# Encoder block on one core: the last round of the second MLP product by plain block products, and first operands loaded in order of use

## The chip, the cores and the metric

The kernel runs on one core of a Trainium2 chip, in one launch. The metric is the device time in microseconds, the median of several executions. Engines: TensorE (PE, with PEld for its weight loads), VectorE (DVE), ScalarE (ACT), GpSimd (POOL) and SyncE (SP), which issues most of the transfers.

## What is computed

The reference is one layer of a hybrid encoder block for 1024 rows of 1024 features in f32: a grouped-query attention branch and a state-space branch, merged and added to x, and then an MLP. Only the end of the MLP is changed here:

```python
h2 = rms_norm(x, norm2_w[l]) * (1.0 + scale2) + shift2
ff = jnp.square(jax.nn.relu(h2 @ w_mlp1[l])) @ w_mlp2[l]
x = x + gate2 * ff
```

`w_mlp1` is 1024 x 4096 and `w_mlp2` 4096 x 1024. The second product thus has 1024 rows, an inner length of 4096 and 1024 columns; each of its rows is gated by column and added to the residual x.

## The kernel before, in words

**Exact products.** An f32 operand is split in two: `hi`, cast by ACT (L169), and `lo`, source less `hi`, by DVE (`tt` in `split`, printed as L155, the line of the helper that records every such operation). A product is then three matmuls: hi by hi, hi by lo, lo by hi (L1672 to L1674 in the second MLP product).

**First MLP product.** The 4096 inner features are 16 pairs `p` of 2 x 128. For each pair the result, 256 features by 1024 rows, is seen as 2 x 2 blocks of 128 x 512 and computed by seven products (`product`, L1331 to L1333) in the manner of Strassen and Winograd, put together by DVE. `keep` applies the squared relu and stores the blocks in DRAM, as `r_d[p][b]`: A11, A12 and A22; POOL forms four sums of blocks, S1 to S4 (`a_sum`), which are stored too.

**Second MLP product.** NR = 4 rounds of KR = 4 pairs. In each round the same seven-product scheme is used, in the order 1, 5, 6, 7, 2, 3, 4: product p takes a block or sum of A (`A_OF`, read back from `r_d`) and a block or sum of the weights, where B11, B12, B21, B22 are read from `w2` and the sums are formed by POOL in place (`SY` is the slot of the sums). A product is 4 steps k (one for each pair of the round) of 4 row blocks t of 3 matmuls, into four PSUM banks, and two sets of four banks take turns. So a round has 7 x 4 x 4 x 3 = 336 matmuls, the whole 1344. In round 0 ACT copies the banks to accumulators `acc[p, t]` (printed as `ac`); in the later rounds DVE adds them. `prepare(n)` makes the two split operands of step n, LA = 2 steps ahead of the matmuls, and sends the next transfers: `a_load` into a ring of 16 tiles `ar`, `load` into the slots `sl`. Split operands (printed as `o`) go round in 12 slots (`op_ring`).

**The end of it.** In the last round `combine` turns the sums of the products into the four output blocks, row half by column half. `gated` multiplies by gate2 and adds the residual tile `xl`, both on POOL for all four blocks (`CE`, "G" each). Where a product is the last of a block, DVE multiplies its bank by the gate into `pg`, adds it, and `finish` sends the tile out.

**The order.** Tiles are allocated from pools with a fixed number of buffers, and a scheduler with a model of the engines fixes the order of the instructions on each engine from the program; a transfer into a reused slot waits for that slot's last reader. The slots `ar` and B12's are those of the first product's operands (pool `act`, 32 of them), so they come free towards its end.

Of the kernel before, what the change touches and what calls it, by code (L numbers as in the profile page):

```python
# [18 lines left out]
P = 128  # L19
# [28 lines left out]
LA = 2  # L48
LA0 = 2
CE = ("GG", "GG", "GG", "GG")  # L50
# [41 lines left out]
def block(ctx: ExitStack, tc: tile.TileContext, ia, out, upto=99, dbg=None):  # L92
# [33 lines left out]
    r_d = [[dram(f"r_{p}_{b}", [P, 512]) for b in range(7)] for p in range(DFF // P // 2)]  # L126
# [1218 lines left out]
    def act_tile(name):  # L1345
        return act.tile([P, 512], F32, name=name, tag="act", bufs=32)

    B11, B21 = act_pairs("b11"), act_pairs("b21")
    with tc.tile_pool(name="p6", bufs=1, reuse_waits="tile") as p6:
# [60 lines left out]
        B22, T1 = act_pairs("b22"), act_pairs("t1")  # L1410
# [19 lines left out]

    with tc.tile_pool(name="p7", bufs=1, reuse_waits="tile") as p7:


        A11, A12, A22, S1, S2, S3, S4 = range(7)
# [19 lines left out]
        def first_two(p, ps1, ps2):  # L1454
            c1 = p7.tile([P, 512], F32, name="c1", tag="c1", bufs=NPRE) if p < NPRE else cu("c1")
# [37 lines left out]
        def load(rd, b, k):  # L1493
            if rd < NR:
                q, h = src[b]
                i = 2 * (rd * KR + k) + q
                dma(blk(b, k), w2[i * P:(i + 1) * P, h * 512:(h + 1) * 512])

        A_OF = {1: A11, 5: S1, 6: S2, 7: S3, 2: A12, 3: S4, 4: A22}
        aloaded = [0]  # L1500
# [9 lines left out]
        ORDER = (1, 5, 6, 7, 2, 3, 4)  # L1510
        steps = [(rd, p, k) for rd in range(NR) for p in ORDER for k in range(KR)]
        ready = {}

        def operand(x, e_lo):
            t = next(op_ring)()
            split(t[:, 0], t[:, 1], x, e_lo=e_lo)
            return t

        def prepare(n):
# [3 lines left out]
            g = lambda b: blk(b, k)  # L1523
            if p == 1:
                b = g(B11_)
            elif p == 5:
                b = g(SY)
                tt(G, b, g(B12_), g(B11_), ALU.subtract)
            elif p == 2:
                b = g(B21_)  # L1530
            elif p == 6:
                b = g(SY)
                tt(G, b, g(B22_), b, ALU.subtract)
            elif p == 7:
                b = g(B12_)
                tt(G, b, g(B22_), b, ALU.subtract)
            elif p == 3:
                b = g(B22_)
            else:
                b = g(B21_)  # L1540
                tt(G, b, g(SY), b, ALU.subtract)
# [20 lines left out]
        raws = {0: load_raw(0)}  # L1562
        for p in range(NP):
# [36 lines left out]
            keep(p, None, b21)  # L1600
# [8 lines left out]
    aring.extend(act_tile("ar") for k in range(4))  # L1609
    for b in (SY, B22_, B21_):  # L1610
        slots[b] = [act_tile("sl") for k in range(KR)]
    for b in (B22_, B21_):
        for k in range(KR):
            load(0, b, k)
    with tc.tile_pool(name="p8", bufs=1, reuse_waits="tile") as p8:
# [7 lines left out]
        def gated(t, h, c, v, e1, e2):  # L1623

            cs = slice(c * 512, (c + 1) * 512)
            xl = p8.tile([P, 512], F32, name="xl", tag="xl", bufs=4)
# [99 lines left out]
```

## Time and profile before

| | us |
|---|---|
| median of 3 runs | 2586.99 (2585.14 to 2591.76) |
| profiled execution | 2585.15 |
| its span | 2583.3 |

The page's mean granted TensorE clock is 0.975. The second MLP product fills the last 355 us of the span, from 2229. A profile is read here by stretches: busy time of an engine in a stretch, then what each of its instructions waited for. A row of the time line gives start, length, engine, line, operation, output and inputs, and in brackets the idle time before it and what ended it. PE's matmuls are pipelined: the distance between two starts is what one costs, not the length printed.

### The profile page before, as it was taken

To read this page: it belongs to the slowest core of one execution; us is meant where nothing else is said; L and a number is where in the kernel's file an instruction comes from. 1 tells how busy PE (TensorE), PEld (TensorE's weight loads), DVE (VectorE), ACT (ScalarE), POOL (GpSimd) and SP (SyncE) were. 2 spreads that over 40 slices of the span, in tenths; PEclk is the share of its full clock that TensorE was granted. 3 is DMA by queue.
4 is the path that set the end of the run, shared out by engine and by line. 5 is a ranking of instruction groups with operands and counts; after the bars stand their busy time and mean duration, and the time that the engine had idled before them with its cause. 6 is when DMAs were issued, how large, how long until landed. Compare 5 with 4: busy or idle time off the path is not lost.

```text
span 2583.3 us, 32423 instructions
## 1 busy us (share of the span) xinstructions
PE 2435.1 (94%) x11355; PEld 1942.7 (75%) x11355; DVE 1835.2 (71%) x2175; ACT 1135.0 (44%) x1968; POOL 1047.2 (41%) x760
## 2 busy tenths in 40 slices
PE   5999999999989999999899999998989999899995
PEld 5898777777767777777577767776867888688884
DVE  5756446888856666666577786557569888768889
ACT  5455423544456666666333444344232222364440
POOL 3210117776611111110356665424028756533356
PEclk9999999999999999999899999999999999899998
DMA  7653751333531212111766665476325443754422
GB/s 262 179 164 123 238 169 59 93 94 91 177 119 58 84 51 95 52 56 37 250 200 193 199 193 172 125 233 208 106 77 178 169 156 139 281 162 152 143 89 98
DMA packets 285619, 369.68 MB, mean 143 GB/s; under 512 B 34057, under 2 KB 166897, under 8 KB 285457
## 3 DMA queue, kind: packets, MB, share of 16 engines
q1 hardware_dynamic: 213873, 292.56, 36.2%
q10 hardware_dynamic: 71584, 75.06, 8.7%
q8 instruction: 90, 1.47, 0.2%
q14 instruction: 72, 0.59, 0.1%
HBM read 251.33 MB, written 116.20 MB: 142 GB/s over the span
## 4 chain that ended last, share of the span: by engine, by line
PE 69%; DVE 11%; DMA 8%; issue 5%; POOL 3%; ACT 3%; SPq 1%; ACTq 0%; DVEq 0%; POOLq 0%
PE pst L905 5%; PE pp L1331 4%; PE pp L1333 4%; PE pp L1332 4%; PE psg L207 4%; PE psg L208 4%; PE psg L209 3%; PE psq L381 3%; PE psq L382 3%; PE psq L380 3%; PE p L1673 3%; PE p L1674 3%; PE p L1672 3%; DVE cacc L714 3%; PE pss L888 2%
## 5 line engine op out<-in xcount | busy, mean ns | idle before, releaser
L892 DVE TENSOR_REDUCE nm<-pss 128x1 f32<-128x1024 f32 x128 | 156.7, 1225 | 134.9 <-PE pss L890 133.4
L381 PE MATMUL psq<-twl,hh 128*128 128x400 f32 (+1 forms) x512 | 193.8, 380 | 5.7 <-DVE twl L155 4.9
L1673 PE MATMUL p<-o,o 128*128 128x512 f32 x448 | 179.6, 401 | 19.2 <-DVE o L155 19.2
L380 PE MATMUL psq<-twh,hh 128*128 128x400 f32 (+1 forms) x512 | 193.4, 383 | 3.3 <-ACT hh L306 1.3
L382 PE MATMUL psq<-twh,hl 128*128 128x400 f32 (+1 forms) x512 | 192.8, 378 | 0.0
L894 ACT ACTIVATE pf<-pss,nm 128x1024 f32<-128x1024 f32 x128 | 142.8, 1116 | 102.0 <-PE pst L905 99.2
L155 DVE TENSOR_TENSOR pl<-pst,ph 128x512 fp32r<-128x512 f32 x256 | 167.9, 683 | 27.7 <-ACT ph L169 27.7
L1672 PE MATMUL p<-o,o 128*128 128x512 f32 x448 | 177.8, 401 | 8.5 <-ACT o L169 8.3
L1674 PE MATMUL p<-o,o 128*128 128x512 f32 x448 | 177.0, 397 | 0.0
L155 POOL TENSOR_TENSOR av<-av,rz 64x512 f32<-64x512 f32 x32 | 41.2, 1288 | 326.7 <-DMA rz<-rz 167.6
L905 PEld LDWEIGHTS pst<-masks,pf 128*128 128x128 f32 x1024 | 118.4, 140 | 69.9 <-issue 29.6
L169 ACT CAST ph<-pst 128x512 fp32r<-128x512 f32 x256 | 146.4, 585 | 54.2 <-PE pst L905 40.9
L905 PE MATMUL pst<-masks,pf 128*128 128x128 f32 x1024 | 157.1, 276 | 11.7 <-DVE pl L155 9.6
L155 POOL TENSOR_TENSOR sl<-sl 128x512 f32<-128x512 f32 x64 | 94.7, 1487 | 176.6 <-DVE o L155 82.2
L714 DVE SCALAR_TENSOR_TENSOR cacc<-pad,cwT,cacc 128x1024 f32<-128x1024 f32 x96 | 162.9, 1727 | 0.4
L169 ACT CAST o<-ar 128x512 fp32r<-128x512 f32 x112 | 69.7, 623 | 175.1 <-PE p L1674 155.8
L155 DVE TENSOR_TENSOR o<-ar,o 128x512 fp32r<-128x512 f32 x112 | 108.1, 965 | 49.3 <-ACT o L169 49.3
L169 ACT CAST wop<-ws 128x512 fp32r<-128x512 f32 x116 | 71.4, 621 | 106.1 <-PE pp L1333 69.2
L1673 PEld LDWEIGHTS p<-o,o 128*128 128x128 f32 x448 | 86.4, 193 | 42.0 <-DVE o L155 24.5
L381 PEld LDWEIGHTS psq<-twl,hh 128*128 128x128 f32 x512 | 99.2, 194 | 17.5 <-DVE twl L155 5.5
L380 PEld LDWEIGHTS psq<-twh,hh 128*128 128x128 f32 x512 | 98.6, 193 | 15.7 <-ACT qkvr L513 1.6
L155 DVE TENSOR_TENSOR o<-sl,o 128x512 fp32r<-128x512 f32 x112 | 108.6, 970 | 0.1
(417 smaller groups left out, 7200.8 us busy)
## 6 DMA issues: line engine op xcount, KB each, us to landing
ar<-r SPq DMA_DIRECT2D x112, 256.0 KB
wada<-in_w_ada_dram SPq DMA_DIRECT2D x48, 512.0 KB
r<-in_w_mlp_dram SPq DMA_DIRECT2D x32, 512.0 KB
r<-as SPq DMA_DIRECT2D x64, 256.0 KB
sl<-in_w_mlp_dram SPq DMA_DIRECT2D x64, 256.0 KB
r<-in_w_in_dram SPq DMA_DIRECT2D x26, 512.0 KB
r<-ro ACTq DMA_DIRECT2D x48, 256.0 KB
xb<-cst ACTq DMA_DIRECT2D x20, 512.0 KB
```

The source lines that it names most:

```text
L155: e.tensor_tensor(out=o, in0=a, in1=b, op=op)
L169: (e_hi or A.copy)(hi, src)
L380: T.matmul(o, hhi[k][half][:, sl], hi[:, k % 2, :n], start=k == 0, stop=False)
L381: T.matmul(o, hhi[k][half][:, sl], lo[:, k % 2, :n], start=False, stop=False)
L382: T.matmul(o, hlo[k][half][:, sl], hi[:, k % 2, :n], start=False, stop=k == KT - 1)
L714: V.scalar_tensor_tensor(out=acc, in0=pad[:, k:k + S], scalar=cwT[:, 24 * k + i:24 * k + i + 1], in1=acc, op0=ALU.mult, op1=ALU.add)
L892: V.tensor_reduce(out=nm, in_=ps, axis=AX.X, op=ALU.max, negate=True)
L894: A.activation(pfs[u], ps, AF.Exp, bias=nm, accum_out=zall[:, u:u + 1])
L905: T.transpose(pt[:, k], pf[:, (hf * 4 + k) * P:(hf * 4 + k + 1) * P], ident)
L1672: T.matmul(pss[t], a[:, 0, sl], b[:, 0], start=k == 0, stop=False)
L1673: T.matmul(pss[t], a[:, 0, sl], b[:, 1], start=False, stop=False)
L1674: T.matmul(pss[t], a[:, 1, sl], b[:, 0], start=False, stop=k == KR - 1)
```

## The change

- The last round uses eight plain block products: for each row half h, inner half q and column half c one, 4 steps of 12 matmuls each, 384 matmuls in place of 336. All eight PSUM banks belong to one row half. The last two of a half's eight steps are done bank by bank, and each bank is finished (gate product, addition, output transfer) as soon as it is full. A fourth block, A21, is kept in `r_d` for the pairs of this round, and their sums S1 to S4 aren't formed.
- `so_far` combines the sums of rounds 0 to 2, applies the gate and adds the residual, on DVE, beside the last round. `gated`, `combine` and `CE` go.
- First operands: four tiles `afirst` in a pool of their own, loaded with B11 during the first product; then B12 and the tiles of the second product in turns, then B22 and those of the third. The sums of weights in round 0 are formed by DVE, in rounds 1 and 2 by POOL. LA is 3. Of the split slots 8 (`HOLD`) are used again for the last round's first weights.

```diff
-LA = 2
+LA = 3
 LA0 = 2
-CE = ("GG", "GG", "GG", "GG")
...
-    r_d = [[dram(f"r_{p}_{b}", [P, 512]) for b in range(7)] for p in range(DFF // P // 2)]
+    r_d = [[dram(f"r_{p}_{b}", [P, 512]) for b in range(8)] for p in range(DFF // P // 2)]
...
-        B22, T1 = act_pairs("b22"), act_pairs("t1")
+        T1, B22 = act_pairs("t1"), act_pairs("b22")
...
+    c1p = ctx.enter_context(tc.tile_pool(name="c1p", bufs=1, reuse_waits="tile"))
...
-        slots, aring = {}, []
+        slots, afirst, aring = {}, [], []
...
+        ORDER = (1, 5, 6, 7, 2, 3, 4)
+        PLAIN = {"00": A11, "01": A12, "10": A21, "11": A22}
+        A_OF = {1: A11, 5: S1, 6: S2, 7: S3, 2: A12, 3: S4, 4: A22, **PLAIN}
+        steps = [(rd, p, k) for rd in range(NR) for p in (ORDER if rd < NR - 1 else PLAIN) for k in range(KR)]
+        aloaded, ready, plain_a, plain_b = [0], {}, {}, {}
+
+        def a_tile(n):
+            return afirst[n] if n < KR else aring[(n - KR) % RING]
 
         def a_load(upto):
 
-            while aloaded[0] < min(upto, len(steps) if len(aring) == RING else len(aring)):
+            while aloaded[0] < min(upto, len(steps) - len(PLAIN) * KR):
                 n = aloaded[0]
                 rd, p, k = steps[n]
-                dma(aring[n % RING], r_d[rd * KR + k][A_OF[p]])
+                dma(a_tile(n), r_d[rd * KR + k][A_OF[p]])
...
+        def plain_load(*names):
+
+            for nm in names:
+                for k in range(KR):
+                    if nm in PLAIN:
+                        plain_a[nm, k] = act_tile("ar")
+                        dma(plain_a[nm, k], r_d[(NR - 1) * KR + k][PLAIN[nm]])
+                    else:
+                        slots[nm][k] = act_tile("sl")
+                        load(NR - 1, nm, k)
...
+            e = V if rd == 0 else G
+            if p in PLAIN:
+                ready[n] = operand(plain_a[p, k], more_slot)
+                if p == "00":
+                    t = [next(held)() for c in range(2)]
+                    plain_b[0, k] = [(t[c][:, 0], t[c][:, 1]) for c in range(2)]
+                elif p == "01":
+                    plain_b[1, k] = [tuple(act_tile("b", F32R) for q in "hl") for c in range(2)]
+                if p[0] == "0":
+                    for c in range(2):
+                        split(*plain_b[int(p[1]), k][c], g(((B11_, B12_), (B21_, B22_))[int(p[1])][c]))
+                if p == "01" and k == KR - 1:
+                    plain_load("10", "11")
+                return
...
-                tt(G, b, g(B12_), g(B11_), ALU.subtract)
+                tt(e, b, g(B12_), g(B11_), ALU.subtract)
...
-            ready[n] = (operand(aring[n % RING], V), operand(b, V))
-            a_load(n + 1 + len(aring))
+                tt(e, b, g(SY), b, ALU.subtract)
+            ready[n] = (operand(a_tile(n), next(op_ring)), operand(b, next(op_ring)))
+            if n >= KR:
+                a_load(n + 1 + RING)
             for f in {5: (B11_,), 7: (B12_,), 3: (B22_,), 4: (B21_,)}.get(p, ()):
-                load(rd + 1, f, k)
+                if rd < NR - 2 or f == B11_:
+                    load(rd + 1, f, k)
+            if rd == NR - 2 and k == KR - 1:
+                plain_load(*{7: ("00", B12_), 4: ("01", B21_, B22_)}.get(p, ()))
...
-            return p8.tile([P, 2, 512], F32R, name="o2", tag="o2", bufs=6)
+            return p8.tile([P, 2, 512], F32R, name="o2", tag="o2", bufs=5)
+
+        def held_slot():
+            return p8.tile([P, 2, 512], F32R, name="o3", tag="o3", bufs=2)
+
+        HOLD = [wp_slot(t) for t in ("whi", "wlo", "whi", "wlo", "wraw", "wraw")] + [held_slot] * 2
 
         def ring():
             while True:
-                for tag in ("whi", "wlo", "whi", "wlo", "wraw", "wraw"):
-                    yield wp_slot(tag)
-                for _ in range(6):
-                    yield more_slot
-
-        op_ring = ring()
+                yield from HOLD
+                yield from [more_slot] * 5
+
+        op_ring, held = ring(), iter(HOLD)
...
-                slots[B12_] = [act_tile("sl") for k in range(KR)]
-                aring.extend(act_tile("ar") for k in range(12))
-                for b in (B11_, B12_):
+                afirst.extend(c1p.tile([P, 512], F32, name="ar", tag="c1", bufs=NPRE) for k in range(KR))
+                for k in range(KR):
+                    load(0, B11_, k)
+                    a_load(k + 1)
+                for f, x in ((B12_, 1), (B22_, 2)):
+                    slots[f] = [act_tile("sl") for k in range(KR)]
+                    aring.extend(act_tile("ar") for k in range(KR))
                     for k in range(KR):
-                        load(0, b, k)
-                a_load(len(aring))
+                        load(0, f, k)
+                        a_load(x * KR + k + 1)
...
-            keep(p, None, b21)
+            keep(p, A21 if p >= NP - KR else None, b21)
+            if p >= NP - KR:
+                b12 = ro()
+                tt(V, b12, u3, product(o4, T4), ALU.subtract)
+                keep(p, A12, b12)
+                continue
...
-    aring.extend(act_tile("ar") for k in range(4))
-    for b in (SY, B22_, B21_):
+    aring.extend(act_tile("ar") for k in range(2 * KR))
+    for b in (SY, B21_):
         slots[b] = [act_tile("sl") for k in range(KR)]
-    for b in (B22_, B21_):
-        for k in range(KR):
-            load(0, b, k)
+    a_load(4 * KR)
+    for k in range(KR):
+        load(0, B21_, k)
+    a_load(KR + RING)
...
+        OUT = {"00": 2, "01": 3, "10": 4, "11": 5}
...
+        def so_far(h, t):
+            ac = lambda p: acc[p, t]
+            if h == "0":
+                tt(V, ac(2), ac(2), ac(1), ALU.add)
+                tt(V, ac(6), ac(6), ac(1), ALU.add)
+                tt(V, ac(3), ac(3), ac(5), ALU.add)
+                tt(V, ac(3), ac(3), ac(6), ALU.add)
+            else:
+                tt(V, ac(7), ac(7), ac(6), ALU.add)
+                tt(V, ac(4), ac(7), ac(4), ALU.subtract)
+                tt(V, ac(5), ac(5), ac(7), ALU.add)
+            for c in "01":
+                v = ac(OUT[h + c])
+                xl = c1p.tile([P, 512], F32, name="xl", tag="c1", bufs=NPRE)
+                dma(xl, x1_d[4 * int(h) + t][:, int(c) * 512:(int(c) + 1) * 512])
+                tt(V, v, v, gate_of(h + c), ALU.mult)
+                tt(V, v, v, xl, ALU.add)
+
+        def finish(h, c, t, ps):
+            v, g = acc[OUT[h + c], t], acc[1, 2 * (t % 2) + int(c)]
+            tt(V, g, ps, gate_of(h + c), ALU.mult)
+            tt(V, v, v, g, ALU.add)
+            r = 4 * int(h) + t
+            dma(out[0][r * P:(r + 1) * P, int(c) * 512:(int(c) + 1) * 512], v)
+
+        first = (NR - 1) % 2
+        for h in "01":
+            pss = [banks(first), banks(1 - first)]
+            ops = []
+            for q in range(2):
+                for k in range(KR):
+                    ops.append((ahead(n), plain_b[q, k]))
+                    n += 1
+                    j = len(ops) - 1
+                    if j < 2 * KR - 2:
+                        for c in range(2):
+                            for t in range(4):
+                                mm(pss[c][t], t, ops[j][0], ops[j][1][c], j == 0, False)
+                    if h == "0" and j < 4:
+                        so_far("0", j)
+                    if h == "0" and j >= 4:
+                        so_far("1", j - 4)
+            for t in range(4):
+                for c in range(2):
+                    for j in (2 * KR - 2, 2 * KR - 1):
+                        mm(pss[c][t], t, ops[j][0], ops[j][1][c], False, j == 2 * KR - 1)
+                    finish(h, "01"[c], t, pss[c][t])```

Three places show what the scheduler made of this. On SP, around the start of the second product: `sl` is a weight block, `ar<-r_b` a first-operand tile of block b (0 is A11, 3 is S1, 4 is S2). Before:

```order
L1497 DMA sl<-in_w_mlp_dram 128x512
L1445 DMA r_6_280<-as 128x512
L1497 DMA sl<-in_w_mlp_dram 128x512 x3
L1507 DMA ar<-r_0_176 128x512
L1507 DMA ar<-r_0_183 128x512
L1507 DMA ar<-r_0_190 128x512
L1507 DMA ar<-r_0_197 128x512
L1507 DMA ar<-r_3_179 128x512
```

Now, at the same place:

```order
L1497 DMA sl<-in_w_mlp_dram 128x512
L1513 DMA ar<-r_3_179 128x512
L1497 DMA sl<-in_w_mlp_dram 128x512
L1513 DMA ar<-r_3_187 128x512
L1497 DMA sl<-in_w_mlp_dram 128x512
L1513 DMA ar<-r_3_195 128x512
L1497 DMA sl<-in_w_mlp_dram 128x512
L1513 DMA ar<-r_3_203 128x512
L1497 DMA sl<-in_w_mlp_dram 128x512
L1513 DMA ar<-r_4_180 128x512
```

The eight weight transfers ahead of the first tile are gone from here, the tiles of A11 come some 80 rows earlier, and weights and tiles alternate.

On DVE, now, at the border of rounds 2 and 3 (helper line L154 here): `p_21216` to `p_21219` are the banks of round 2's last product, `o_21284<-ar` and the next three rows of that form are low parts of the last round's first operands, `o<-sl` those of its weights.

```order
L154 TENSOR_TENSOR o_21341<-sl,o_21341 128x512
L154 TENSOR_TENSOR o_21342<-sl,o_21342 128x512
L154 TENSOR_TENSOR ac<-ac 128x512 x2
L154 TENSOR_TENSOR ac<-ac,p_21216 128x512
L154 TENSOR_TENSOR o_21284<-ar,o_21284 128x512
L154 TENSOR_TENSOR o_21305<-ar,o_21305 128x512
L154 TENSOR_TENSOR ac<-ac,p_21217 128x512
L154 TENSOR_TENSOR ac<-ac,p_21218 128x512
L154 TENSOR_TENSOR ac<-ac,p_21219 128x512
L154 TENSOR_TENSOR o_21338<-ar,o_21338 128x512
L154 TENSOR_TENSOR o_21383<-ar,o_21383 128x512
```

The splits of eight weight tiles of each of two halves, and the first parts of `so_far`, now stand among the additions that free the banks.

On PE, now, at the end of row half 0 (`p_21330` and `p_21334` are two of the eight banks, `b` the weights, `o_21477` and `o_21524` the last two steps' first operands):

```order
L1672 MATMUL p_21330<-b,o_21477 128x512
L1673 MATMUL p_21330<-b,o_21477 128x512
L1674 MATMUL p_21330<-b,o_21477 128x512
L1672 MATMUL p_21330<-b,o_21524 128x512
L1673 MATMUL p_21330<-b,o_21524 128x512
L1674 MATMUL p_21330<-b,o_21524 128x512
L1672 MATMUL p_21334<-b,o_21477 128x512
```

Six matmuls close a bank before the next bank is begun; before, the four banks of a product were closed within the same step, three matmuls apart.

## Rows read from the trace of the kernel before

**Rows 1.** The page: busy time by engine, and the chain that ended last.

```profile
PE 2435.1 (94%) x11355; PEld 1942.7 (75%) x11355; DVE 1835.2 (71%) x2175; ACT 1135.0 (44%) x1968; POOL 1047.2 (41%) x760
...
PE 69%; DVE 11%; DMA 8%; issue 5%; POOL 3%; ACT 3%; SPq 1%; ACTq 0%; DVEq 0%; POOLq 0%
```

**Rows 2.** Windows: length, busy PE, PEld, DVE, ACT, POOL, clock, DMA share, GB/s.

```profile
2229.00:2257.00 28.00, 19.24 (x62) 14.13 (x61) 21.63 (x22) 10.24 (x19) 21.15 (x14) 0.76 0.96 337
2257.00:2521.00 264.00, 264.00 (x1166) 218.60 (x1165) 205.75 (x260) 122.66 (x218) 101.39 (x68) 1.00 0.45 139
2521.00:2584.00 63.00, 35.64 (x121) 25.21 (x119) 59.38 (x62) 5.70 (x10) 43.19 (x25) 0.82 0.29 100
```

**Rows 3.** Matmuls into the product's banks, 2262 to 2520: first and last starts.

```profile
L1672 PE MATMUL p<-o,o x380: 389/389/390, 2261.8 to 2519.5; 128*128 128x512 f32 x190
...
L1674 PE MATMUL p<-o,o x380: 388/389/390, 2262.2 to 2520.0; 128*128 128x512 f32 x190
```

**Rows 4.** Time line of PE at the start of the second product.

```profile
2229.19 0.39 PE L1672 MATMUL p<-o,o 128*128 128x512 f32 x1
...
2234.53 0.80 PE L1672 MATMUL p<-o,o 128*128 128x512 f32 x1 [1.93 <-ACT o L169]
2235.12 0.63 PE L1673 MATMUL p<-o,o 128*128 128x512 f32 x1
2235.55 0.63 PE L1672 MATMUL p<-o,o 128*128 128x512 f32 x1
...
2248.07 2.07 PE L1672 MATMUL p<-o,o 128*128 128x512 f32 x4 [6.36 <-ACT o L169]
...
2253.96 1.43 PE L1672 MATMUL p<-o,o 128*128 128x512 f32 x4
```

**Rows 5.** Time line of ACT there: the casts that waited for transfers.

```profile
2233.86 0.62 ACT L169 CAST o<-ar 128x512 fp32r<-128x512 f32 x1 [6.59 <-DMA sl<-in_w_mlp_dram]
...
2239.84 0.62 ACT L169 CAST o<-ar 128x512 fp32r<-128x512 f32 x1 [5.36 <-DMA ar<-r]
```

**Rows 6.** Time line of SP's queue there: first weight block, first tiles.

```profile
2210.55 0.33 SPq L1497 DMA_DIRECT2D sl<-in_w_mlp_dram  x1
...
2220.67 6.29 SPq L1507 DMA_DIRECT2D ar<-r  x12
```

**Rows 7.** Time line of PE in the tail.

```profile
2529.61 0.50 PE L1673 MATMUL p<-o,o 128*128 128x512 f32 x1 [3.67 <-DVE o L155]
...
2548.85 0.80 PE L1673 MATMUL p<-o,o 128*128 128x512 f32 x1 [2.89 <-DVE o L155]
...
2555.55 0.79 PE L1673 MATMUL p<-o,o 128*128 128x512 f32 x1 [3.77 <-DVE o L155]
...
2575.20 0.39 PE L1674 MATMUL p<-o,o 128*128 128x512 f32 x1
```

**Rows 8.** Time line of DVE in the last round.

```profile
2491.95 1.79 DVE L155 TENSOR_TENSOR o<-ar,o 128x512 fp32r<-128x512 f32 x1
2493.66 1.78 DVE L155 TENSOR_TENSOR o<-sl,o 128x512 fp32r<-128x512 f32 x1
...
2498.77 1.87 DVE L155 TENSOR_TENSOR ac<-ac,p 128x512 f32<-128x512 f32 x3
...
2509.14 0.68 DVE L155 TENSOR_TENSOR ac<-ac,p 128x512 f32<-128x512 f32 x1
2509.74 0.68 DVE L155 TENSOR_TENSOR o<-ar,o 128x512 fp32r<-128x512 f32 x1
...
2579.10 1.28 DVE L155 TENSOR_TENSOR ac<-ac,pg 128x512 f32<-128x512 f32 x2
```

**Rows 9.** Time line of POOL there; it is idle from 2508.07 to 2511.10.

```profile
2491.43 5.16 POOL L155 TENSOR_TENSOR ac<-ac,gate 128x512 f32<-128x512 f32 x3
```

**Rows 10.** DVE groups, 2258 to 2480: busy us, mean ns, idle before.

```profile
L155 DVE TENSOR_TENSOR o<-ar,o 128x512 fp32r<-128x512 f32 x82 | 73.9, 901 | 42.8 <-ACT o L169 42.8
L155 DVE TENSOR_TENSOR o<-sl,o 128x512 fp32r<-128x512 f32 x82 | 67.1, 818 | 0.0
```

More of the change, by code (lines that the diff above doesn't have):

```diff
@@ L1343, in act_pairs, with act_tile @@
         return [tuple(act.tile([P, 512], F32R, name=f"{name}{q}_{j}", tag="act", bufs=32) for q in "hl") for j in range(HK)]
-    def act_tile(name):
-        return act.tile([P, 512], F32, name=name, tag="act", bufs=32)
+    def act_tile(name, dt=F32):
+        return act.tile([P, 512], dt, name=name, tag="act", bufs=32)
     B11, B21 = act_pairs("b11"), act_pairs("b21")
@@ L1454, in first_two @@
         def first_two(p, ps1, ps2):
-            c1 = p7.tile([P, 512], F32, name="c1", tag="c1", bufs=NPRE) if p < NPRE else cu("c1")
+            c1 = c1p.tile([P, 512], F32, name="c1", tag="c1", bufs=NPRE) if p < NPRE else cu("c1")
             A.copy(c1, ps1)
@@ L1493, in load, with operand @@
         def load(rd, b, k):
[L1494 to L1500, printed above, removed]
+            q, h = src[b]
+            i = 2 * (rd * KR + k) + q
+            dma(blk(b, k), w2[i * P:(i + 1) * P, h * 512:(h + 1) * 512])
+        ORDER = (1, 5, 6, 7, 2, 3, 4)
[5 more added lines that the diff above has]
+            return afirst[n] if n < KR else aring[(n - KR) % RING]
         def a_load(upto):
-            while aloaded[0] < min(upto, len(steps) if len(aring) == RING else len(aring)):
+            while aloaded[0] < min(upto, len(steps) - len(PLAIN) * KR):
                 n = aloaded[0]
                 rd, p, k = steps[n]
-                dma(aring[n % RING], r_d[rd * KR + k][A_OF[p]])
+                dma(a_tile(n), r_d[rd * KR + k][A_OF[p]])
                 aloaded[0] += 1
[L1510 to L1516, printed above, removed]
+        def plain_load(*names):
[7 more added lines that the diff above has]
+                        load(NR - 1, nm, k)
+        def operand(x, slot):
+            t = slot()
+            split(t[:, 0], t[:, 1], x)
             return t
@@ L1659, in block, with banks, mm @@
-        n, done = 0, LA0
-        for rd in range(NR):
-            last = rd == NR - 1
+        def banks(first):
+            return [ps7.tile([P, 512], F32, name="p2", tag=("ps1", "ps2")[first], bufs=4) for t in range(4)]
+        def mm(ps, t, a, b, start, stop):
+            sl = slice(t * P, (t + 1) * P)
+            T.matmul(ps, a[:, 0, sl], b[0], start=start, stop=False)
+            T.matmul(ps, a[:, 0, sl], b[1], start=False, stop=False)
+            T.matmul(ps, a[:, 1, sl], b[0], start=False, stop=stop)
@@ L1662, in block, with ahead @@
+        done = [LA0]
+        def ahead(n):
+            for m in range(max(done[0], n), n + LA + 1):
+                prepare(m)
+            done[0] = max(done[0], n + LA + 1)
+            return ready.pop(n)
+        n = 0
+        for rd in range(NR - 1):
             for i, p in enumerate(ORDER):
-                pss = [ps7.tile([P, 512], F32, name="p2", tag=("ps1", "ps2")[i % 2 if rd % 2 == 0 else 1 - i % 2], bufs=4) for t in range(4)]
+                pss = banks((i + rd) % 2)
                 for k in range(KR):
-                    for m in range(max(done, n), min(n + LA + 1, len(steps))):
-                        prepare(m)
-                    done = max(done, n + LA + 1)
-                    a, b = ready.pop(n)
+                    a, b = ahead(n)
@@ L1669, in block @@
                     n += 1
                     for t in range(4):
-                        sl = slice(t * P, (t + 1) * P)
-                        T.matmul(pss[t], a[:, 0, sl], b[:, 0], start=k == 0, stop=False)
-                        T.matmul(pss[t], a[:, 0, sl], b[:, 1], start=False, stop=False)
-                        T.matmul(pss[t], a[:, 1, sl], b[:, 0], start=False, stop=k == KR - 1)
+                        mm(pss[t], t, a, (b[:, 0], b[:, 1]), k == 0, k == KR - 1)
                 for t in range(4):
-                    v, ps = acc[p, t], pss[t]
@@ L1677, in block, with gate_of @@
                     if rd == 0:
-                        A.copy(v, ps)
-                    elif not last or p in (1, 5, 6, 7):
-                        tt(V, v, v, ps, ALU.add)
-                    if last:
-                        combine(p, t, v, ps)
+                        A.copy(acc[p, t], pss[t])
+                    else:
+                        tt(V, acc[p, t], acc[p, t], pss[t], ALU.add)
+        OUT = {"00": 2, "01": 3, "10": 4, "11": 5}
+        def gate_of(hc):
+            return gate2[:, int(hc[1]) * 512:(int(hc[1]) + 1) * 512]
```

40 lines of the change are left out of this document (5 added, 35 removed).

## The prediction

> **What bounds the kernel now.** I read the page's busy line first: TensorE 94% of the span, and the chain that ended last is 69% TensorE and 11% VectorE [rows 1]. Shares over the whole span hide stages, so the next view is the table by stretches [rows 2]. It cuts the second MLP product in three: a start of 28 us in which TensorE is busy for 19.24 us at a granted clock of 0.76 with the DMA engines 0.96 full; a middle of 264 us without a gap at clock 1.00; and a tail of 63 us in which TensorE is busy for 35.64 us at 0.82 while VectorE is busy for 59.38. The middle is TensorE's. The tail is VectorE's. The start belongs to transfers.
>
> In the middle the three matmul lines have 380 instructions each, the first at 2261.8 and the last at 2520.0 [rows 3]: 258.2 us over 1139 steps, 0.2267 us per matmul. All 1344 would take 304.7 us at this rate. They begin at 2229.19 [rows 4], so the last would end at 2533.9. It starts at 2575.20 [rows 7] and is through by about 2575.4: **41.5 us are lost inside the product**.
>
> Where? At the start 48 matmuls are done at 2253.96, where 48 steps would have ended at 2240.1: 13.9 us lost, in one wait of 1.93 and one of 6.36 us and in matmuls at 0.43 instead of 0.2267 us (2235.12 to 2235.55) behind each [rows 4]. The wait of 6.36 names ScalarE, which had itself waited 6.59 us for a weight block and 5.36 us for a first-operand tile [rows 5]: SyncE sent twelve of these tiles in one piece from 2220.67, behind the weights that it had begun to send at 2210.55 [rows 6]. From 2253.96 to 2520.9 there are 267 us, or 1177 steps, so 1225 are done there (the tail's window shows 121, two of them begun before). The 119 left would take 27.0 us; they take until 2575.4: **27.5 us lost in the tail**, in waits of 2.89 to 3.77 us for VectorE's `o` [rows 7]. VectorE is slow there because POOL works too: an operation with two operands in SBUF comes every 1.71 us (2491.95 to 2493.66) while POOL runs its gate products at the same rate, and every 0.60 us (2509.14 to 2509.74) when POOL is idle; three additions that read PSUM take 1.87 us beside POOL, 0.62 each [rows 8, 9]. Last come VectorE's pairs behind the last matmul, to 2580.38 [rows 8]; the span ends 2.9 us later.
>
> **The change, part by part.**
> Matmuls: the last round goes from 7 x 48 = 336 to 8 x 48 = 384. 48 more at 0.2267 are **+10.9 us**, in full on the path, since TensorE is the bound. 1392 x 0.2267 = 315.6.
>
> Start: four first-operand tiles and B11 are fetched during the first product. Then weights B12 and B22 alternate with the tiles of the next two steps: 16 transfers of 256 KB from 2210.5. At the 337 GB/s of the start [rows 2] one takes 0.78 us, all 12.4, so they are there by 2223. Steps 4 to 7, the first to use them, begin at 2229.2 + 4 x 12 x 0.2267 = 2240.1: 17 us of cover. Without it the old waits come back (rival 1). The block sums of round 0 move from POOL to VectorE, 16 operations at 0.60 = 9.6 us over a round of 336 x 0.2267 = 76 us; VectorE has room. What is late next is the second step's low part: some 14 VectorE operations at 0.60 stand ahead of it, which makes it ready about 0.4 us after TensorE wants it; I put 0.9 to the steps behind it, where casts and subtractions follow each other as closely. I take **1.3 us** of the 13.9; bounds 0 (all hidden) and 6 (one wait as long as the 6.36 seen [rows 4]).
>
> Preparing three steps ahead, not two, costs no instructions. Sixteen S sums on POOL and their stores (four for each of four pairs) fall away, during the first product; POOL isn't its bound, so nothing.
>
> Border of rounds 2 and 3: here VectorE gets crowded. From the moment the fourth-last product of round 2 starts to be drained (32.6 us, or 144 matmuls, before the border) its order holds 63 operations up to the addition that frees the first of the last product's banks. 63 x 0.60 = 37.8 us, 5.2 behind the border; that addition ends at 5.8. TensorE's order comes to that bank 20 matmuls = 4.5 us behind the border: 1.3 us late. Four POOL sums still fall into this stretch, and each makes one or two VectorE operations cost 1.71 instead of 0.60 [rows 8, 9]: 2 to 4 us on top, of which part is regained since other matmuls stand ready. I take **3.5 us**. Bounds: 0 (VectorE ahead by then) and 8 (all of it, and two matmul steps at 0.43). The twelve weight and operand transfers for the round come into a stretch where the DMA engines are 0.45 full [rows 2]; hidden, unless the slots come free too late (rival 2).
>
> Last round: POOL has nothing, so VectorE pays 0.60. From that addition to the end it has 88 operations, 53 us, in 87 us of TensorE. Combining rounds 0 to 2, the gate and the residual: hidden, with 34 us to spare. A bank is drained by two operations (1.2 us) while TensorE fills the next with 6 matmuls (1.36 us): hidden but for the last. The tail's 27.5 us go, and the 5 us between the last matmul and VectorE's end shrink to 0.2 + 1.3 (one pair, as the last one here [rows 8]). The output's transfer behind it stays, 2.9.
>
> By the Trainium skill (Perfetto Trace Analysis, Matmuls under Optimizing Tensor Performance) independent groups should rotate through banks so that draining one overlaps the next group's matmuls; all eight banks now belong to one half, so by that rule the draining is exposed. Rival 4 is what this would make of the time.
>
> **Sum.** 2229.2 + 315.6 + 1.3 + 3.5 = 2549.6; + 0.2 + 1.3 + 2.9 = 2554.0 against a span of 2583.3. The profiled execution took 2585.15, 1.85 more than its span, so 2555.9; the median of the runs, 2586.99, lies 1.84 above it: **2558 us**, 29 less. The other way round: -12.6 (start) -27.5 (tail) -3.5 (last pairs) +10.9 +3.5 = -29.2.
>
> **Rivals.**
> 1. *The start stays as it is*: ScalarE or VectorE, not transfers, set it. For: both waits name them [rows 4]. Against: ScalarE's own waits end with transfers [rows 5]. 12.6 more: 2570.5.
> 2. *The round's twelve late transfers hold the border.* Slots come free one by one as the last products are prepared, and their casts stand in line on ScalarE and VectorE. For: a transfer in line cost 6.59 and 5.36 us at the start [rows 5]; two such waits are 12. Against: DMA is half empty then. 2558 + 12 = 2570.
> 3. *VectorE stays slow in round 2*: its operations cost the mean of rounds 0 to 3 (0.901 and 0.818, so 0.86 [rows 10]) and not 0.60. 64 x 0.86 = 55.0, so the bank is free 22.4 behind the border and not 5.8: 14 to 17 more, 2573. Against: those means hold twice the POOL sums that are left, and the gate work.
> 4. *Draining is exposed*, 8 banks x 1.2 us at each half's end, less the one pair counted: 18 more, 2576. Against: six matmuls stand between two drains, and the next half begins with the bank drained first.
> 5. *Slower*: VectorE paces the last round from wait to wait, and TensorE, idling before each step, is granted its lower level, as behind the two waits of the start now: 0.43 instead of 0.2267, 1.2 instead of 2.4 GHz [rows 4]. 384 x 0.2 = 77 more: 2635. It cancels the gain from 29 / 0.2 = 145 matmuls on, or when VectorE's 151 operations from 32.6 us before the border on cost 1.01 us instead of 0.60 (32.6 + 87 + 3.5 + 29 = 152 us). For: it has just that price beside POOL. Against: POOL has no work in that round. The Trainium skill (TensorE: Matmul & The Clock Gate, HAM oscillation) tells of the same loss between bursts of matmuls, and the 0.82 of the tail [rows 2] agrees.
>
> That the change doesn't do what it says I exclude: the instruction orders show it.
>
> **Chances.** Forecast 0.77; rival 1 0.05; rival 2 0.06; rival 3 0.04; rival 4 0.03; rival 5 0.05. Measurement tells 0.3% (7.8 us) from no change. Faster therefore holds the forecast and rivals 1 to 4, each of which leaves 11 us or more; two of them together would land within 0.3%, and I take 0.05 off for this. Faster 0.90, same 0.05, slower 0.05. Range: the stalls' bounds give 2553 to 2567 about 2558; 4 us below for a border and an end better than counted and for the spread of the runs, and the single rivals above: **2549 to 2575**.
>
> **What would show it.** Right: no POOL work behind the last round's begin; `o` at 0.60 us pitch; TensorE's first 48 matmuls done by about 2241.5; clock 1.00 up to the end; at the border one wait of a few us for VectorE's addition; one pair of VectorE operations behind the last matmul. Wrong: waits of over 2 us in every step of the last round, a second wait for transfers behind the border, or matmuls at 0.43 us for longer than one step. The forecast falls if the tail's waits return in another place.

## The result

The changed kernel takes 2553.88 us (median of 4 runs, 2551.91 to 2555.1), the kernel before beside it 2586.06 (4 runs, 2579.48 to 2591.76): a ratio of 0.9876, 95% interval 0.9851 to 0.99. That is 32 us less, where 29 were forecast, and inside the range. The profiled execution took 2555.1 us with a span of 2553.3, where the sum gave 2555.9 and 2554.0.

### The profile after

The page, span and busy line, answering to [rows 1]:

```profile
span 2553.3 us, 32339 instructions
...
PE 2422.2 (95%) x11403; PEld 1935.0 (76%) x11403; DVE 1779.8 (70%) x2199; ACT 1121.7 (44%) x1944; POOL 908.8 (36%) x672
```

48 more matmuls, and 88 fewer operations on POOL. The windows, cut at the round's border and behind the last matmuls, with the columns of [rows 2]:

```profile
2229.00:2257.00 28.00, 27.19 (x118) 21.55 (x117) 23.35 (x40) 17.80 (x34) 0.00 (x0) 1.00 0.86 291
2257.00:2460.00 203.00, 203.00 (x897) 168.11 (x896) 156.40 (x226) 99.39 (x177) 49.61 (x32) 1.00 0.47 145
2460.00:2546.00 86.00, 84.60 (x374) 69.71 (x373) 55.90 (x92) 8.01 (x13) 0.00 (x0) 1.00 0.21 71
```

Both holes are closed: TensorE is busy for 27.19 of the first 28 us (19.24 before), and for 84.60 of 86 us where the tail was. POOL, busy for 21.15 and 43.19 us in these two stretches before, has nothing there. All waits of TensorE in the product that are over 0.1 us are the three in brackets here, on its time line:

```profile
2229.96 0.39 PE L1672 MATMUL p<-o,o 128*128 128x512 f32 x1
...
2233.11 1.20 PE L1672 MATMUL p<-o,o 128*128 128x512 f32 x4 [0.25 <-ACT o L168]
...
2240.53 0.50 PE L1673 MATMUL p<-o,o 128*128 128x512 f32 x1 [0.55 <-DVE o L154]
...
2250.64 0.39 PE L1672 MATMUL p<-o,o 128*128 128x512 f32 x1
...
2464.39 0.39 PE L1673 MATMUL p<-o,o 128*128 128x512 f32 x1
2466.18 0.50 PE L1672 MATMUL p<-o,o 128*128 128x512 f32 x1 [1.40 <-DVE ac L154]
...
2548.61 0.39 PE L1674 MATMUL p<-b,o 128*128 128x512 f32 x1
```

The row at 2250.64 is the 85th matmul. 84 steps of 0.2267 us are 19.04, it comes 20.68 behind the first: 1.6 us lost at the start, where the kernel before lost 14.2 by the same count. The wait of 1.40 is the border's. On VectorE's time line it ends with the addition from the last product's first bank, and the end of the kernel reads:

```profile
2465.44 0.68 DVE L154 TENSOR_TENSOR ac<-ac,p 128x512 f32<-128x512 f32 x1
...
2539.51 0.69 DVE L154 TENSOR_TENSOR ac<-p,gate 128x512 f32<-128x512 f32 x1 [16.33 <-PE p L1674]
...
2549.03 0.69 DVE L154 TENSOR_TENSOR ac<-p,gate 128x512 f32<-128x512 f32 x1
2549.76 0.69 DVE L154 TENSOR_TENSOR ac<-ac 128x512 f32<-128x512 f32 x1
```

VectorE waits 16.33 us for the last half's first bank: it is the bound no more. One pair of operations stands behind the last matmul, to 2550.45, and the span ends 2.85 us later.

### One table for all runs

The second product began between 2225.3 and 2234.9 us in the 14 profiles, whatever was changed in it; this moves a run's time by several us. So each run below, by its one profile, is also measured from its own first matmul: *start* is the loss over the first 84 (as above), *rest* is the span's end less the first matmul, less 304.7 us (1344 steps), less the start's loss. The rest holds the tail, the end and, with plain blocks, 10.9 us for 48 more matmuls.

| run | median, us | start | rest |
|---|---|---|---|
| before | 2584 to 2586 | 14.2 | 35.2 |
| changed | 2553.9 | 1.6 | 17.0 |
| start's edits alone | 2582.5 | 11.8 | 35.2 |
| end's edits alone | 2560.1 | 5.5 | 17.0 |
| before, combination on VectorE | 2571.8 | 14.5 | 24.7 |
| changed, gate on POOL | 2563.0 | 1.7 | 25.7 |
| changed, no draining bank by bank | 2559.5 | 1.6 | 20.7 |
| changed, block sums on POOL | 2557.7 | 7.1 | 17.0 |
| changed, S sums kept | 2561.3 | 9.2 | 17.0 |
| changed, old order of loads | 2554.3 | 1.6 | 17.0 |
| changed, two steps ahead | 2553.9 | 1.7 | 17.0 |
| start's edits, stores from SyncE | 2578.7 | 9.5 | 35.2 |
| S sums kept, stores from SyncE | 2560.5 | 8.9 | 17.0 |
| start's edits and combination on VectorE | 2568.7 | 11.5 | 22.7 |

An edit inside one of the two stretches moves the other column by 0.2 us at most; the last run is the exception, with a rest of 22.7 against 24.7 (see its place below). Where "end's edits alone" changes the start, the S sums that it drops do it, as tested below. Two of the expectations below give 6.9 and 9.0 for losses that are 7.1 and 9.2 by the row of the 85th matmul.

### The profile page after: what moved, and what is told of

The parts are those of the page before. It is cut to its first block, busy times and chain, and to the rows that moved or that the text cites. A ratio compares the mean times of both kernels' runs of the same rounds, so it can differ in the third digit from the quotient of the medians.

```text
span 2553.3 us, 32339 instructions
## 1 busy us (share of the span) xinstructions
PE 2422.2 (95%) x11403; PEld 1935.0 (76%) x11403; DVE 1779.8 (70%) x2199; ACT 1121.7 (44%) x1944; POOL 908.8 (36%) x672
## 5 line engine op out<-in xcount | busy, mean ns | idle before, releaser
L154 DVE TENSOR_TENSOR pl<-pst,ph 128x512 fp32r<-128x512 f32 x256 | 167.9, 683 | 27.6 <-ACT ph L168 27.6
L168 ACT CAST ph<-pst 128x512 fp32r<-128x512 f32 x256 | 146.4, 585 | 54.2 <-PE pst L904 41.0
L154 POOL TENSOR_TENSOR av<-av,rz 64x512 f32<-64x512 f32 x32 | 41.3, 1290 | 326.5 <-DMA rz<-rz 158.5
L1673 PE MATMUL p<-o,o 128*128 128x512 f32 x400 | 155.2, 389 | 0.6 <-DVE o L154 0.6
L1672 PE MATMUL p<-o,o 128*128 128x512 f32 x400 | 153.8, 390 | 1.7 <-DVE ac L154 1.4
L1674 PE MATMUL p<-o,o 128*128 128x512 f32 x400 | 153.8, 389 | 0.0
L168 ACT CAST wop<-ws 128x512 fp32r<-128x512 f32 x116 | 71.7, 621 | 103.6 <-PE pp L1332 67.5
L154 POOL TENSOR_TENSOR sl<-sl 128x512 f32<-128x512 f32 x32 | 49.6, 1553 | 178.5 <-DVE o L154 72.4
L381 PEld LDWEIGHTS psq<-twh,hl 128*128 128x128 f32 x512 | 97.8, 191 | 11.9 <-issue 0.9
L1106 ACT ACTIVATE e<-psd 128x512 f32<-128x512 f32 x128 | 70.8, 595 | 74.6 <-PE psd L1104 61.4
L168 ACT CAST o<-sl 128x512 fp32r<-128x512 f32 x92 | 56.9, 623 | 105.0 <-PE p L1674 88.4
L941 PE MATMUL pv<-pl,v 128*64 128x512 f32 x256 | 102.0, 419 | 0.0
```

What stands on the lines that cost most here:

```text
L154: e.tensor_tensor(out=o, in0=a, in1=b, op=op)
L168: (e_hi or A.copy)(hi, src)
L381: T.matmul(o, hlo[k][half][:, sl], hi[:, k % 2, :n], start=False, stop=k == KT - 1)
L1672: T.matmul(ps, a[:, 0, sl], b[0], start=start, stop=False)
L1673: T.matmul(ps, a[:, 0, sl], b[1], start=False, stop=False)
L1674: T.matmul(ps, a[:, 1, sl], b[0], start=False, stop=stop)
```

## The experiments

### The two parts, each alone

The first takes the edits of the start into the kernel before (`afirst`, the order of the loads, `e = V if rd == 0 else G`, LA = 3). The sums S1 to S4 have to stay, since its last round reads them.

> The kernel before with the start of the change alone (first tiles early, loads in order of use, block sums of round 0 on VectorE, three steps ahead); its last round is as before. Theory (the two parts are worth what the stretches lost): the first 48 matmuls of the second product are done 13 us sooner, the tail keeps its 27.5 us, so 2586 - 13 = 2573 us (2570 to 2576). Rival A (the start's wait only moves behind the first steps): no wait of 6.36 us at the first 48 matmuls but waits of as much later in round 0, 2584 to 2588. Rival B (the whole gain comes with the end): 2586.

2582.53 us (2577.11 to 2585.95), ratio 0.999 (0.998 to 0.9999). The start still loses 11.8 us: neither the theory's 1 us nor a wait that moved behind it, but nearly the old waits, for ScalarE's casts:

```profile
2235.39 0.50 PE L1683 MATMUL p<-o,o 128*128 128x512 f32 x1 [2.43 <-ACT o L169]
...
2247.80 2.07 PE L1683 MATMUL p<-o,o 128*128 128x512 f32 x4 [6.63 <-ACT o L169]
```

The second takes the edits of the start out of the changed kernel:

> The changed kernel with the start of the kernel before (old order of the loads, block sums of round 0 on POOL, two steps ahead); the last round stays plain. Theory: 13 us of waits come back at the start and nothing else, 2554 + 13 = 2567 us (2563 to 2570), with waits of about 2 and 6 us in the first 48 matmuls. Rival (the plain last round frees slots so that the start hardly counts): 2554 to 2557. If the two parts add up, this run and the one with the start alone lose together what the change gains, 32 us.

2560.08 us (2558.14 to 2563.95). The start loses 5.5, not 14. So the two parts don't add up as written: the edits meant for the start bring 2.4 us on their own, and taking them out costs 3.9. 8.7 us of the start's gain come with the plain last round. What of it could reach 230 us ahead?

### What the start's gain is made of

The plain last round reads no S sums, and the last pair's four fall just into the start. They stand on POOL's time line of the kernel before, as rows `as`, among the block sums `sl`:

```profile
2233.36 1.27 POOL L155 TENSOR_TENSOR as<-ro 128x512 f32<-128x512 f32 x1 [1.23 <-DVE ro L1438]
2234.57 5.96 POOL L155 TENSOR_TENSOR sl<-sl 128x512 f32<-128x512 f32 x4
2241.87 1.64 POOL L155 TENSOR_TENSOR sl<-sl 128x512 f32<-128x512 f32 x1 [1.33 <-DVE o L155]
2243.47 1.71 POOL L155 TENSOR_TENSOR as<-as,ro 128x512 f32<-128x512 f32 x1
2245.14 1.70 POOL L155 TENSOR_TENSOR as<-ro 128x512 f32<-128x512 f32 x1
...
2248.04 1.74 POOL L155 TENSOR_TENSOR as<-ro,as 128x512 f32<-128x512 f32 x1
```

Four runs take one thing each out of the changed kernel. The S sums are kept (nobody reads them):

```diff
-            if p >= NP - KR:
-                b12 = ro()
-                tt(V, b12, u3, product(o4, T4), ALU.subtract)
-                keep(p, A12, b12)
-                continue
```

> The changed kernel, but POOL goes on forming the sums S1 to S4 of the last four pairs and storing them, though nobody reads them. Theory (the last pair's sums fall into the start of the second product: POOL slows VectorE there, and their stores stand in the line of transfers): the loss over the first 84 matmuls goes from 1.6 to 8 to 12 us, 2561 to 2565. Rival (the prediction's own step: POOL is no bound in the first product, so these sums cost nothing): 1.6 us, 2554.

Loss 9.2 us, 2561.31 us (2558.66 to 2568.34): **7.6 us for the sums** that the prediction put at nothing, with these waits:

```profile
2236.05 0.79 PE L1667 MATMUL p<-o,o 128*128 128x512 f32 x1 [5.31 <-ACT o L168]
...
2246.02 0.50 PE L1668 MATMUL p<-o,o 128*128 128x512 f32 x1 [0.54 <-DVE o L154]
```

The block sums of round 0 go back to POOL:

```diff
-            e = V if rd == 0 else G
+            e = G
```

> The changed kernel with one edit: the block sums of round 0 go back from VectorE to POOL. Theory (POOL beside VectorE makes VectorE's subtractions take 1.7 us where the first steps have no lead): the loss over the first 84 matmuls, 1.6 us in the changed kernel, becomes 4 to 8, 2556 to 2561. Rival (POOL has time, VectorE is relieved): 1.6 us or less, 2554.

Loss 7.1 us, 2557.74 us (2554.83 to 2559.19): **5.5 us for the block sums**, with these waits:

```profile
2233.55 0.50 PE L1672 MATMUL p<-o,o 128*128 128x512 f32 x1 [2.08 <-ACT o L168]
...
2243.03 0.80 PE L1673 MATMUL p<-o,o 128*128 128x512 f32 x1 [2.81 <-DVE o L154]
```

Together 13.1, a little more than the start's 12.6, but this isn't a division of the gain: the two overlap. With the S sums in place, block sums on VectorE, the new order and the third step together bring 2.4 us only (14.2 to 11.8). The order of the loads, then, as in the kernel before (B11 and B12, twelve tiles, B22 and B21):

> The changed kernel with the loads of the start alone as before (weights B11 and B12, then twelve tiles, then B22 and B21); block sums of round 0 on VectorE, three steps ahead and no sums S1 to S4 for the last pairs, as in the changed kernel. Loss over the first 84 matmuls: 1.6 us in the changed kernel, 5.5 with the old loads, POOL's block sums and two steps ahead together. Theory A (the order of the loads is what is left of the gain): 4 to 6 us. Theory B (the sums on VectorE carry it, since with POOL's sums alone the loss was 6.9): 1 to 3 us. The rest of the product stays at 17 us: 2555 to 2558.

Loss 1.6 us, 2554.34 us (2550.54 to 2557.33), as much as in the changed kernel, with two waits of 0.51: theory A falls. **The order of the loads, which the change is named for, is worth nothing** once POOL is out of the way. And LA = 2:

> The changed kernel preparing two steps ahead, not three, and nothing else. Theory (the lead costs nothing and gives little where VectorE has its list in the same order): loss at the start 1.6 to 3 us, rest 17 us, 2554 to 2556. Rival (the third step is what covers the first waits): a loss of 4 to 7, 2557 to 2560.

Loss 1.7 us, 2553.9 us (2549.86 to 2561.06): nothing either. That holds without POOL in the start; with its block sums there, the old order and two steps ahead lose 5.5 (end's edits alone), the new order and three steps 7.1.

### Why ScalarE's casts were late

[Rows 5] name transfers for the casts' waits. But ScalarE's queue has something between: the row ahead of each cast there is a store's issue.

```profile
2233.41 0.33 ACTq L1440 DMA_DIRECT2D r<-ro  x1
...
2239.39 0.33 ACTq L1440 DMA_DIRECT2D r<-ro  x1
```

They are the stores of the last pair's blocks (`adma` in `keep`), and the program makes each wait for an earlier transfer's counter beside VectorE's result, as the instruction's list of waits in the program has it:

```
L1440 DMA r_15_2_283<-ro_19335 128x512 [waits DMAHW5_49,DVE_49]
L169 CAST o2_19351<-ar_19242 128x512 [waits DMAHW1_49,PE_49,Activation_49]
```

The counter of this store is raised by a weight transfer to `sl`, that of the next one by a first-operand transfer to `ar`: the transfers that [rows 5] name are those for which the stores waited. VectorE had the two blocks ready before, at 2229.28 and 2236.89:

```profile
2227.50 1.78 DVE L1438 SCALAR_TENSOR_TENSOR ro<-ro 128x512 f32<-128x512 f32 x1
...
2235.12 1.77 DVE L1438 SCALAR_TENSOR_TENSOR ro<-ro 128x512 f32<-128x512 f32 x1
```

So in a full line (DMA 0.96 busy) the stores stood 4.1 and 2.5 us longer than their data asked for, and the casts behind them. The Trainium skill (DMA: Bandwidth & Descriptors, Anatomy of one DMA — SWDGE (gpsimd) path) says that a transfer's wait happens on the issuing sequencer, not in the DMA engines. These rows agree. Two runs move the stores to SyncE's queue, one from the start's edits alone, one from the run with the S sums kept:

```diff
-                adma(r_d[p][b], c)
+                (dma if p == NP - 1 else adma)(r_d[p][b], c)
```

> The run with the start of the change alone, which still lost 11.8 us over the first 84 matmuls, with one edit more: the stores of the last pair's blocks are issued by SyncE and not by ScalarE. Theory (ScalarE's casts stand behind a store that waits for an earlier transfer of the line to land): the casts are free of it, and the loss falls to 2 to 6 us. Rival A (the casts wait for their own tiles): 10 to 12 us stay. Rival B (SyncE now stands behind these stores, and the loads come late): a loss of 10 us or more with the casts waiting for ar or sl.

> The run that kept the sums S1 to S4, with the last pair's blocks stored from SyncE's queue and not from ScalarE's. It lost 9.0 us over the first 84 matmuls, with one wait of 5.31 us for a cast that stood behind two such stores on ScalarE. Theory (the stores wait for an earlier transfer of the line, the casts for the stores): that wait goes and the loss falls to 2 to 5 us. Rival A (the casts wait for their own tiles): 8 to 10 us. Rival B (SyncE is held up by the stores instead, and the tiles come late): 5 to 9 us, with casts waiting for ar or sl.

The losses go from 11.8 to 9.5 and from 9.2 to 8.9 only; the theory's numbers are missed in both. The time line of ScalarE in the run with the S sums kept, and then with its stores on SyncE:

```profile
2232.24 3.04 ACTq L1440 DMA_DIRECT2D r<-ro  x2
2235.38 1.14 ACT L168 CAST o<-ar 128x512 fp32r<-128x512 f32 x2 [9.47 <-DMA ar<-r]
```

```profile
2231.86 0.62 ACT L168 CAST o<-ar 128x512 fp32r<-128x512 f32 x1 [2.11 <-PE p L1669]
2236.29 1.24 ACT L168 CAST o<-sl 128x512 fp32r<-128x512 f32 x2 [3.80 <-DVE sl L154]
```

The wait of 9.47 is gone with the stores, so they made most of it (without them the same two casts wait 2.17 and 2.11 us, for TensorE); no cast there waits for its tile. But behind them ScalarE waits 3.80 us for a block sum by VectorE, and TensorE 1.87 and 3.22 us. On VectorE's time line of the same run, with POOL at the S sums from 2228.4 to 2235.0:

```profile
2229.79 1.80 DVE L154 TENSOR_TENSOR o<-ar,o 128x512 fp32r<-128x512 f32 x1
2231.51 1.78 DVE L1438 SCALAR_TENSOR_TENSOR ro<-ro 128x512 f32<-128x512 f32 x1
2233.22 4.79 DVE L154 TENSOR_TENSOR sl<-sl 128x512 f32<-128x512 f32 x6
```

Eight operations take 8.1 us, where 0.60 each would be 4.8. And the block sums come late: the first begin 4.3 us behind TensorE's first matmul (2228.93), in the changed kernel 3.4 us ahead of it (2229.96):

```profile
2226.55 1.29 DVE L154 TENSOR_TENSOR sl<-sl 128x512 f32<-128x512 f32 x2
```

So a second delay lay under the first. The changed kernel leaves the stores on ScalarE, and one of them stands ahead of a cast that waits 4.39 us, but TensorE then waits only the 0.25 us shown above:

```profile
2232.02 0.33 ACTq L1440 DMA_DIRECT2D r<-ro  x1
2232.44 0.62 ACT L168 CAST o<-ar 128x512 fp32r<-128x512 f32 x1 [4.39 <-DVE o L154]
```

How much of the 7.6 us is POOL beside VectorE, how much the stores' longer line and how much the order that the scheduler then chooses stays open.

### The end: POOL beside VectorE

In the kernel before, all of `combine`'s 40 POOL operations go to VectorE; seven products stay:

```diff
-CE = ("GG", "GG", "GG", "GG")
+CE = ("VV", "VV", "VV", "VV")
...
-                tt(G, acc[2, t], acc[2, t], v, ALU.add)
+                tt(V, acc[2, t], acc[2, t], v, ALU.add)
...
-                tt(G, acc[3, t], acc[3, t], v, ALU.add)
+                tt(V, acc[3, t], acc[3, t], v, ALU.add)
```

> The kernel before with one thing changed: the 40 gate products, residual and other additions of the last round that POOL does are given to VectorE. Theory (VectorE is slow in the tail because POOL works at the same time): VectorE has 101 + 40 operations from 2480 on, at 0.60 instead of a mean of 1.05 us 85 us instead of 106, so the tail shortens by 10 to 20 us: 2566 to 2576 us. Rival (VectorE has too much to do, POOL beside it costs nothing): 40 more operations at its mean of 1.05 us make the tail 42 us longer, 2628 us.

2571.8 us (2570.92 to 2575.74), ratio 0.9955 (0.994 to 0.997); the rest falls from 35.2 to 24.7. VectorE does 40 operations more and the end comes 10.5 us sooner, counted from the product's begin and without the start's loss. Its time line there:

```profile
2540.12 0.68 DVE L155 TENSOR_TENSOR o<-ar,o 128x512 fp32r<-128x512 f32 x1
2540.72 0.68 DVE L155 TENSOR_TENSOR ac<-ac,gate 128x512 f32<-128x512 f32 x1
2541.32 0.68 DVE L155 TENSOR_TENSOR ac<-ac 128x512 f32<-128x512 f32 x1
```

0.60 us from start to start, as in [rows 8] with POOL idle. The other way round, in the changed kernel:

```diff
-                tt(V, v, v, gate_of(h + c), ALU.mult)
-                tt(V, v, v, xl, ALU.add)
+                tt(G, v, v, gate_of(h + c), ALU.mult)
+                tt(G, v, v, xl, ALU.add)
```

> The changed kernel with the 32 gate products and residual additions beside the last round given back to POOL. Theory (POOL beside VectorE slows both): VectorE's operations beside them take 1.7 instead of 0.60 us; those that fall ahead of the border make the wait there grow from 1.4 us to 4 to 8; behind it VectorE has more than 30 us to spare, so little more: 2556 to 2562 us. Rival (taking work off VectorE helps): the wait of 1.4 us at the border goes, 2552 to 2553.

2563.0 us (2562.82 to 2566.42); the rest grows from 17.0 to 25.7. VectorE has 32 operations fewer; beside POOL its operations come 1.71 us apart again, and the border's wait goes from 1.40 to 6.12:

```profile
2474.95 0.80 PE L1672 MATMUL p<-o,o 128*128 128x512 f32 x1 [6.12 <-DVE ac L154]
2475.55 0.63 PE L1673 MATMUL p<-o,o 128*128 128x512 f32 x1
2475.97 0.63 PE L1674 MATMUL p<-o,o 128*128 128x512 f32 x1
```

```profile
2456.47 1.78 DVE L154 TENSOR_TENSOR o<-sl,o 128x512 fp32r<-128x512 f32 x1
2458.18 1.79 DVE L154 TENSOR_TENSOR o<-ar,o 128x512 fp32r<-128x512 f32 x1
```

This is within the 4 to 8 of the theory; with the matmuls behind it at 0.43 us instead of 0.2267 (2475.55 to 2475.97) the border costs 10.2 us in all, more than the theory's total. The rival, that VectorE is relieved, falls.

The draining, with the last two steps over all eight banks like the others:

```diff
-                    if j < 2 * KR - 2:
+                    if j < 2 * KR:
```

(and the matmuls of the last two steps taken out of the loop that finishes the banks).

> The changed kernel, but the last two steps of a half go over all eight banks like the others, so that the banks are closed three matmuls (0.68 us) apart and not six (1.36 us). Theory (VectorE drains a bank in 1.3 us): it falls 0.65 us behind per bank, 5 us over eight; at the end all of that is exposed, between the halves 0 to 5 of it: 5 to 10 us more, 2559 to 2564. Rival (the whole draining is exposed at both halves, as rival 4 of the prediction priced it): 18 us more, 2572. Rival (VectorE keeps up anyway): 2554.

2559.46 us (2557.32 to 2560.34). The rest is 20.7: 3.7 us more, below the 5 to 10 expected and far from rival 4's 18. All of it lies at the end; VectorE's first and last row and TensorE's last row there:

```profile
2545.80 1.37 DVE L154 TENSOR_TENSOR ac<-p,gate 128x512 f32<-128x512 f32 x2 [21.09 <-PE p L1674]
...
2554.28 1.29 DVE L154 TENSOR_TENSOR ac<-ac 128x512 f32<-128x512 f32 x2
```

```profile
2550.14 0.39 PE L1674 MATMUL p<-b,o 128*128 128x512 f32 x1
```

VectorE's 16 operations run without a pause from the first bank on, and end 5.4 us behind the begin of the last matmul and not 1.8. Between the halves TensorE doesn't wait at all.

Last, are plain blocks needed once POOL is out of the way? The start's edits and `combine` on VectorE, with seven products:

> The kernel before with both the start's edits and the combination on VectorE; the last round keeps its seven products. Theory (start and rest add up): start 11.8 us lost as with the start's edits alone, the rest 24.6 us as with the combination on VectorE, against 1.6 and 17.0 in the changed kernel: 2571 us or so, slower than the changed kernel by 15 to 18 us. Rival (without POOL's gate work the seven products need no plain blocks, 48 matmuls or 10.9 us fewer): 2550 to 2556.

2568.72 us (2567.22 to 2570.65): start 11.5, rest 22.7. The columns nearly add up again; the 1.9 us less than 24.7 match a wait of 1.84 us for a residual tile `xl` at the end of that run, which this one, with `xl` in another pool, doesn't have. Seven products on VectorE leave 22.7 and eight plain ones 17.0, 48 matmuls included; the plain blocks also let the S sums go. TensorE's and VectorE's last rows with seven products:

```profile
2552.02 0.39 PE L1685 MATMUL p<-o,o 128*128 128x512 f32 x1
```

```profile
2563.34 1.32 DVE L155 TENSOR_TENSOR ac<-ac,pg 128x512 f32<-128x512 f32 x2
```

VectorE, at 0.60 and with POOL idle, ends 12.4 us behind the last matmul's step. So POOL's absence is only a part of the tail's gain. From 35.2 the rest falls to 6.1 without the 10.9 for 48 matmuls, by 29.1 us; moving the combination to VectorE gives 10.5 to 12.5 of them, the plain last round with its bank by bank end the other 16.6 to 18.6. No run beats the changed kernel by what can be told.

## Why the prediction came out

**Right, with its mechanism.** *Matmuls*: the last half runs at 0.2267 without a wait, 48 more cost 10.9. *Last round*: VectorE at 0.60 with POOL idle, hidden, and TensorE's clock at 1.00. The reason given for the tail, that VectorE is slow because POOL works too, is a part of it (10.5 to 12.5 of 29.1 us); the rest came with the plain last round as a whole, in which VectorE combines the earlier rounds beside the matmuls and not behind them. Of that whole the runs separate only the bank by bank end (3.7 us). *End*: VectorE is done 1.6 us behind the last matmul's step (counted 0.2 + 1.3), and the span ends 2.85 later (counted 2.9). *Draining*: hidden; without the bank by bank order 3.7 us, so rival 4 was priced too high.

**Right in size, wrong in cause: the start.** 12.6 us were counted and 12.6 came; that the number fits is luck. The step said that transfers set the start, that fetching in order of use takes the waits away, and that VectorE merely has room for the block sums. The order of loads is worth nothing; each taken alone out of the changed kernel, the block sums on VectorE are worth 5.5 us and the S sums 7.6, which the step "POOL isn't its bound, so nothing" had dismissed. That step asked whether POOL ends the stage. It should have asked who works beside POOL, and where the last pair's sums lie: [rows 2] had POOL busy for 21.15 of the start's 28 us, and I read DMA's 0.96 beside it. Rival 1 came nearer to the mechanism (ScalarE and VectorE set the start) and drew the wrong conclusion, that the change would leave it. Transfers had their part, but through the stores that waited for them, not through the casts' own tiles.

**Right in place, too large: the border.** The wait came 20 matmuls behind the border, for the very addition foretold; it cost 1.7 us in all and not 3.5. The surcharge of 2 to 4 us for POOL's sums was the error: POOL's last one ended at 2428.3, before nearly all of this stretch:

```profile
2424.36 1.62 POOL L154 TENSOR_TENSOR sl<-sl 128x512 f32<-128x512 f32 x1 [1.89 <-DVE o L154]
2426.66 1.62 POOL L154 TENSOR_TENSOR sl<-sl 128x512 f32<-128x512 f32 x1 [0.68 <-POOL sl L154]
```

From 2430 to 2466 VectorE's operations come 0.60 us apart (each row 0.68 long), its price alone. The plain count, 1.3, was nearer.

**Rivals 2, 3 and 5** didn't come: no wait for a transfer at the border, VectorE at 0.60 and not 0.86 there, no matmul at 0.43 in the last round.

**The sum.** The product began 0.8 us later than counted and lost 1.5 less at the start and the border together (3.3 against 4.8), so the span's 2554.0 came out as 2553.3. The median is 4 us under the forecast because the profiled execution was the slowest of the four, where the sum had added 1.84 us for the reverse.

## What to carry to other kernels

When two parts of a change fall on the same stretch, a sum that comes out right doesn't show which one did it; take them out one at a time, and measure from the stretch's own first instruction, since the stages ahead moved by up to 10 us here. Work on POOL isn't priced at nothing because POOL has time: ask what VectorE does beside it, where an operation with two operands in SBUF cost 1.71 us instead of 0.60 here. And where a cast waits for a transfer, look at what stands ahead of it on its own queue before believing the name.

## What the runs showed of the hardware

That 32 operations fewer on VectorE made the kernel 9 us slower, and 40 more made it 12 us faster, has the sign that the theories gave it, the first a little more than foretold: moving work between the two engines cost or gave 0.27 and 0.26 us for each operation, in the rest column (8.7 / 32 and 10.5 / 40). Not expected was the store: in the run with the S sums kept, a wait of 9.47 us stood before a cast behind two issues on ScalarE's queue, and without them the casts' own tiles gave no wait at all.
